# Four norms between the layers of a one-core kernel: pinned sums and spread, the residual feature by feature

## The chip, the core and the metric

The kernel runs on one core of one Trainium2 chip. The metric is the time of the device in microseconds for one execution. Engines are named as in the profile: PE (TensorE), DVE (VectorE), ACT (ScalarE), POOL (GpSimd) and SP (SyncE, which issues nearly all DMAs).

## The reference, cut to what matters

One batch of 512 tokens with 1024 features goes through four layers, the first two with 16 further tokens in front: a gated delta rule, a latent attention, a mixer of dilated attention and pooling, and a feed-forward layer. Each ends in an output projection, and behind each projection stands the same norm with a residual:

```python
def rmsnorm(x, g):
    xf = x.astype(jnp.float32)
    y = xf * lax.rsqrt(jnp.mean(xf * xf, axis=-1, keepdims=True) + NORM_EPS)
    return (y * g.astype(jnp.float32)).astype(x.dtype)
...
        h = h + rmsnorm(y, post_norm[layer])
```

The next layer starts with a norm of h and projections of it.

## The kernel before

All activations lie feature by feature: a partition is one of 128 features of a tile, eight tiles make the 1024 features, and tokens run along the free dimension, in two halves (272 and 256 tokens in the first joins' layer, 256 and 256 later). Every fp32 value is cut into a high and a low part (`hi` on ACT, `lo` on DVE or POOL, lines 70 to 80), and every product is three matmuls (lines 66 to 68): high by high, low by high, high by low. Weights come as raw tiles over SP and are cut in the same way (`whi` on ACT, `wlo` mostly on DVE).

A `Mix` is an output projection with its norm. There are four: of w_out (layer 1), w_out of layer 2, w_out of layer 3, and w_down. I call the passages behind the first three join 1, 2 and 3, and that behind w_down the end. A Mix runs column tile by column tile (m, eight of them) and half by half (i). ACT squares the result into `ysq` (line 339), POOL adds it to `acc` (line 341; the last tile's add is DVE's), and ACT writes the scaled result to `y` (line 342).

The norm of one half is `token_rs`: the sums, small matmuls of `acc` with ones (line 440); mean and eps on DVE (`v`, line 443); the power on POOL (line 446); a diagonal `dg` per 128 tokens on DVE (line 453); the spread, a matmul of ones with `dg` that puts a token's factor into all partitions (line 456); and a copy of it to SBUF, `rs`, on ACT (line 457). Then `residue` multiplies each feature of `y` by `rs` (line 367, even features on DVE, odd on POOL), adds the residual `resid` (line 369), and hands it to the next layer (`intake`: high and low part, scaled by the next norm's gain, as `h1hi`/`h1lo`, `x2hi`/`x2lo`, `x3hi`/`x3lo`). SP stores h to DRAM in two parts (line 375). Squares of h are added for the next norm (lines 467 to 471; POOL in half 0, DVE in half 1).

The residual of a half is one load of 1 MB (line 353) into one buffer: half 1's can start only when half 0's adds have read it.

While half 0 of a Mix is normed, PE goes on with column tiles of half 1. Sums and spread are issued by `Side`, a queue of steps with due times: each step of products moves its clock on by the time that PE should take (`PASS`), and a step that is due is traced at that place. `NORM_AFTER` and `NORM_GAP` are the due times of sums and spread in microseconds. In joins 2 and 3 the next layer's first four column tiles (PSUM tiles `first`) start early: `early()` runs them on half 0, one unit after another, and `late()` on half 1. The real order on each engine is set by a scheduler that simulates a timeline and takes instructions by readiness and priority; only what is marked with `keep_in_program_order` keeps its traced place.

Of the kernel before, what the change touches and what calls it, by code (L numbers as in the profile page):

```python
# [56 lines left out]
NORM_AFTER, NORM_GAP = 0.9, 2.0  # L57
# [7 lines left out]
def split_mm(nc, ps, whi, wlo, xhi, xlo, start, stop):  # L65
    nc.tensor.matmul(ps, lhsT=whi, rhs=xhi, start=start, stop=False)  # L66
    nc.tensor.matmul(ps, lhsT=whi, rhs=xlo, start=False, stop=False)  # L67
    nc.tensor.matmul(ps, lhsT=wlo, rhs=xhi, start=False, stop=stop)  # L68
# [136 lines left out]
def tile_model(ctx, tc, a, out):  # L205
# [7 lines left out]
    e.side = Side()  # L213
# [78 lines left out]
class Mix:  # L292
# [31 lines left out]
    def tile_parts(self, m, i, ks):  # L324
# [4 lines left out]
        for k, (hi, lo) in enumerate(ks):  # L329
            split_mm(nc, ps[:, :n], hi, lo, self.xhi[i][:, k], self.xlo[i][:, k], k == 0, k == len(ks) - 1)  # L330
# [6 lines left out]
        else:  # L337
            sq = pool.tile([P, self.hv[0].stop], F32, tag="ysq", name="ysq", bufs=2)
            nc.scalar.activation(sq[:, :n], ps[:, :n], AF.Square)  # L339
            eng = nc.vector if m == order[-1] else nc.gpsimd  # L340
            eng.tensor_tensor(out=acc[:, s], in0=acc[:, s], in1=sq[:, :n], op=ALU.add)  # L341
# [13 lines left out]
    def norm(self, i, nxt):  # L355
        e = self.e
        s = self.hv[i]
        rs = self.pool2.tile([P, self.hv[0].stop], F32, tag="rs", name="rs")[:, :s.stop - s.start]
        token_rs(e, rs, self.acc, s, D, NORM_AFTER, lambda: self.residue(i, nxt, rs), gap=NORM_GAP)

    def residue(self, i, nxt, rs):
        e, nc, y, x = self.e, self.e.nc, self.y[i], self.x[i]
        s = self.hv[i]
        n = s.stop - s.start
        for k in range(KT):
            eng = nc.gpsimd if k % 2 else nc.vector
            eng.tensor_tensor(out=y[:, k], in0=y[:, k], in1=rs, op=ALU.mult)  # L367
            eng = nc.gpsimd if nxt is None and k % 4 == 3 else nc.vector
            eng.tensor_tensor(out=y[:, k], in0=y[:, k], in1=x[:, k, :n], op=ALU.add)  # L369
            if nxt is None:  # L370
                nc.sync.dma_start(e.out[:, k, s], y[:, k])
            else:
                nxt.intake(k, i, s, y[:, k])
                if k % 4 == 3:
                    nc.sync.dma_start(self.h_dram[:, k - 3:k + 1, s], y[:, k - 3:k + 1])
        if nxt is not None:
            for k in range(KT):
                sum_squares(e, nxt.pool, nxt.acc, k, s, y[:, k])

# [1752 lines left out]
```

## Time and profile before

| | us |
|---|---|
| median of 3 runs | 1693.45 |
| lowest, highest run | 1687.04, 1695.97 |
| profiled execution | 1688.91 |
| its span, first to last instruction | 1687.1 |

| engine | busy us | share of the span |
|---|---|---|
| PE | 1592.0 | 94% |
| DVE | 992.4 | 59% |
| ACT | 836.1 | 50% |
| POOL | 470.9 | 28% |

The mean granted clock of TensorE over the span is 0.982. The joins lie at about 585 to 670, 1040 to 1097 and 1284 to 1331 us of the span, the end from 1655 on. A timeline row gives start and duration of a run of instructions and, in brackets, the idle time of the engine before it and what ended it; a row of waits gives the instruction that waited, what it waited for, the total, the number of times and the longest. A window's row gives the busy time of each engine in that stretch, with its number of instructions, and the granted clock.

### The profile page before, as it was taken

The numbers are of one execution on the slowest core, as the hardware profiler recorded it, in microseconds if no ns is written. First come the engines' busy times: TensorE is split into PE (matmuls) and PEld (weight loads), VectorE is DVE, ScalarE is ACT, GpSimd is POOL, SyncE is SP. The second block draws the span as 40 slices with busy tenths as digits, with TensorE's granted clock in tenths as the row PEclk, the third lists the DMA queues.
The fourth block names the chain that finished last, engine by engine and source line by source line (L and its number), as shares of the span: only waits on it lengthen the run. The fifth ranks groups of instructions, "written<-read, shape, count | busy, mean of one in ns | idle before, by whom it ended". The sixth has DMA issues, their size and how long they took to land.

```text
span 1687.1 us, 32900 instructions
## 1 busy us (share of the span) xinstructions
PE 1592.0 (94%) x12564; PEld 1456.0 (86%) x12564; DVE 992.4 (59%) x1944; ACT 836.1 (50%) x2005; POOL 470.9 (28%) x684
## 2 busy tenths in 40 slices
PE   6999869999999988999999999899998999999996
PEld 6999768888789988878999899788888888888996
DVE  6847749655365476785676623677855655554233
ACT  4876545544586553334666533435764433322230
POOL 1112110110286552122434312343535211111113
PEclk9999989999999998999999999999999999999998
DMA  3257963424466553456221223376624222223332
GB/s 134 95 174 209 199 153 123 119 85 157 132 178 197 176 193 105 142 186 192 59 76 48 73 94 132 119 233 192 159 69 140 88 94 94 100 98 105 98 113 76
DMA packets 133362, 219.72 MB, mean 130 GB/s; under 512 B 35989, under 2 KB 81365, under 8 KB 133077
## 3 DMA queue, kind: packets, MB, share of 16 engines
q1 hardware_dynamic: 126436, 204.83, 39.5%
q10 hardware_dynamic: 6768, 12.79, 2.1%
q8 instruction: 99, 1.62, 0.4%
q14 instruction: 59, 0.48, 0.1%
HBM read 173.81 MB, written 42.45 MB: 128 GB/s over the span
## 4 chain that ended last, share of the span: by engine, by line
PE 73%; DMA 8%; DVE 8%; issue 5%; ACT 4%; POOL 2%; SPq 1%; DVEq 0%; POOLq 0%; ACTq 0%
PE pj_t L66 19%; PE pj_t L67 19%; PE pj_t L68 19%; DMA bca<-row_a 2%; DMA item_dram<-bca 2%; DVE wlo L75 2%; DVE y L369 1%; DMA raw<-w_z 1%; DMA item<-item_dram 1%; DVE y L367 1%; PE ptr L1665 1%; PE ks L1234 1%; PE o_ps L1272 1%; PE sc L66 1%; PE ks L1233 1%
## 5 line engine op out<-in xcount | busy, mean ns | idle before, releaser
L75 DVE TENSOR_TENSOR wlo<-raw,whi 128x1024 fp32r<-128x1024 f32 (+2 forms) x218 | 290.5, 1334 | 239.2 <-ACT whi L74 238.6
L74 ACT ACTIVATE whi<-raw 128x1024 fp32r<-128x1024 f32 (+3 forms) x225 | 232.4, 1033 | 346.9 <-PE pj_t L67 205.1
L66 PE MATMUL pj_t<-hhi,whi 128*128 128x272 f32 (+2 forms) x760 | 224.3, 297 | 6.1 <-ACT y L665 1.9
L67 PE MATMUL pj_t<-hlo,whi 128*128 128x272 f32 (+2 forms) x760 | 223.8, 295 | 0.0
L68 PE MATMUL pj_t<-hhi,wlo 128*128 128x272 f32 (+2 forms) x760 | 223.2, 294 | 0.0
L66 PEld LDWEIGHTS pj_t<-hhi,whi 128*128 128x128 f32 (+1 forms) x760 | 145.2, 191 | 9.7 <-issue 2.6
L68 PEld LDWEIGHTS pj_t<-hhi,wlo 128*128 128x128 f32 (+1 forms) x760 | 145.0, 191 | 6.1 <-issue 5.5
L67 PEld LDWEIGHTS pj_t<-hlo,whi 128*128 128x128 f32 (+1 forms) x760 | 145.3, 191 | 2.5 <-issue 1.7
L68 PE MATMUL pj_t<-x3hi,wlo 128*128 128x512 f32 x320 | 124.6, 389 | 0.0
L66 PE MATMUL pj_t<-x3hi,whi 128*128 128x512 f32 x320 | 124.6, 389 | 0.0
L67 PE MATMUL pj_t<-x3lo,whi 128*128 128x512 f32 x320 | 124.5, 389 | 0.0
L341 POOL TENSOR_TENSOR acc<-acc,ysq 128x256 f32<-128x256 f32 (+1 forms) x48 | 58.4, 1217 | 194.8 <-ACT ysq L339 194.7
L68 PE MATMUL pj_t<-ahi,wlo 128*128 128x256 f32 x352 | 99.1, 282 | 0.0
L66 PE MATMUL pj_t<-ahi,whi 128*128 128x256 f32 x352 | 99.1, 282 | 0.0
L67 PE MATMUL pj_t<-alo,whi 128*128 128x256 f32 x352 | 99.0, 281 | 0.0
L1343 POOL TENSOR_SCALAR p<-p,st 128x144 f32<-128x144 f32 (+3 forms) x112 | 61.8, 553 | 132.5 <-DVE st L1342 91.4
L2022 POOL TENSOR_TENSOR gt<-gt,x3rs 128x512 f32<-128x512 f32 x22 | 30.1, 1368 | 191.6 <-DVE gt L2021 191.6
L68 PE MATMUL pj_t<-ghi,wlo 128*128 128x272 f32 (+1 forms) x256 | 74.1, 289 | 4.5 <-DVE wlo L75 4.5
L66 PE MATMUL pj_t<-ghi,whi 128*128 128x272 f32 (+1 forms) x256 | 75.8, 296 | 0.0
L1334 ACT ACTIVATE p<-p,st 128x144 f32<-128x144 f32 (+3 forms) x112 | 63.2, 564 | 23.2 <-DVE st L1329 21.1
L67 PE MATMUL pj_t<-h1lo,whi 128*128 128x512 f32 (+2 forms) x192 | 70.9, 370 | 3.4 <-DVE h1lo L75 2.9
L669 DVE SCALAR_TENSOR_TENSOR y<-xpad,fixed,y 128x528 f32<-128x528 f32 x96 | 73.4, 766 | 0.6
(551 smaller groups left out, 4797.0 us busy)
## 6 DMA issues: line engine op xcount, KB each, us to landing
raw<-w_out SPq DMA_DIRECT2D x54, 512.0 KB, 3.6
raw<-w_z SPq DMA_DIRECT2D x32, 512.0 KB, 3.3
item<-item_dram SPq DMA_DIRECT2D x32, 384.0 KB, 3.2
raw<-w_v SPq DMA_DIRECT2D x22, 512.0 KB, 4.0
raw<-w_gate SPq DMA_DIRECT2D x22, 512.0 KB, 3.2
raw<-w_up SPq DMA_DIRECT2D x22, 512.0 KB, 3.3
sz<-sz_dram SPq DMA_DIRECT2D x64, 128.0 KB, 2.7
raw<-w_down SPq DMA_DIRECT2D x16, 512.0 KB, 3.5
```

Of the source, the lines that this page charges most:

```text
L66: nc.tensor.matmul(ps, lhsT=whi, rhs=xhi, start=start, stop=False)
L67: nc.tensor.matmul(ps, lhsT=whi, rhs=xlo, start=False, stop=False)
L68: nc.tensor.matmul(ps, lhsT=wlo, rhs=xhi, start=False, stop=stop)
L74: nc.scalar.activation(hi, src, AF.Copy)
L75: (engine or nc.vector).tensor_tensor(out=lo, in0=src, in1=hi.bitcast(F32), op=ALU.subtract)
L341: eng.tensor_tensor(out=acc[:, s], in0=acc[:, s], in1=sq[:, :n], op=ALU.add)
L367: eng.tensor_tensor(out=y[:, k], in0=y[:, k], in1=rs, op=ALU.mult)
L369: eng.tensor_tensor(out=y[:, k], in0=y[:, k], in1=x[:, k, :n], op=ALU.add)
L669: nc.vector.scalar_tensor_tensor(out=y, in0=xpad[:, j:j + T1], scalar=cw[:, tap0, j:j + 1], in1=y, op0=ALU.mult, op1=ALU.add)
L1334: nc.scalar.activation(p[:, :at], p[:, :at], AF.Exp, bias=st[:, len(sc) - 1:len(sc)], scale=-1.0, accum_out=st[:, 3:4])
L1343: nc.gpsimd.tensor_scalar(out=p[:, :n], in0=p[:, :n], scalar1=st[:, 2:3], scalar2=factor, op0=ALU.mult, op1=ALU.mult)
L2022: nc.gpsimd.tensor_tensor(out=gt, in0=gt, in1=rs, op=ALU.mult)
```

## The change

Sums and spread of these norms are pinned: their matmuls, and the first matmul of the product behind them, keep the place on PE at which `Side` traced them, and both steps run at a raised priority (`NORM_EARLY`), as do the last column tile's square and add. `NORM_AFTER` goes from 0.9 to 1.3 and `NORM_GAP` from 2.0 to 2.2. ACT no longer copies the spread: the multiplications read it in PSUM, except in half 0 of the first Mix, where the copy stays.

`residue` becomes `features`: for each feature a multiplication, an add and (on ACT) the high part, then the low part of the feature before. All of it that is not ACT's is on DVE, in program order; POOL does none of it. In half 0 of the first Mix one feature is traced every 3.4 us (`FEATURE`) of the side queue's time; elsewhere all eight at once. `early` and `late` run the four first units feature by feature: all four with feature 0, then all four with feature 1. Their weights are taken before the last held tile of half 0.

```diff
-NORM_AFTER, NORM_GAP = 0.9, 2.0
+NORM_AFTER, NORM_GAP = 1.3, 2.2
+NORM_EARLY = 400
+FEATURE = 3.4
...
+    def place(self, ins):
+
+        self.tc.keep_in_program_order(ins)
+        self.held = True
+
+    def hold(self, ins):
+        if self.held:
+            self.tc.keep_in_program_order(ins)
+            self.held = False
...
+            last = m == order[-1]
+            with self.e.tc.high_priority(offset=NORM_EARLY if last else 0):
...
-        rs = self.pool2.tile([P, self.hv[0].stop], F32, tag="rs", name="rs")[:, :s.stop - s.start]
-        token_rs(e, rs, self.acc, s, D, NORM_AFTER, lambda: self.residue(i, nxt, rs), gap=NORM_GAP)
+        rs = None
+        if self.keep is None and i == 0:
+            rs = self.pool2.tile([P, CUT], F32, name="rs")[:, :s.stop - s.start]
...
+        steps = self.features(i, nxt, rs)
+        if self.keep is None and i == 0:
+            for j in range(KT + 1):
+                self.e.side.add(FEATURE * j, lambda: next(steps))
...
         for k in range(KT):
-            eng = nc.gpsimd if k % 2 else nc.vector
-            eng.tensor_tensor(out=y[:, k], in0=y[:, k], in1=rs, op=ALU.mult)
-            eng = nc.gpsimd if nxt is None and k % 4 == 3 else nc.vector
-            eng.tensor_tensor(out=y[:, k], in0=y[:, k], in1=x[:, k, :n], op=ALU.add)
+            in_order(nc.vector.tensor_tensor(out=y[:, k], in0=y[:, k], in1=rs, op=ALU.mult))
+            in_order(nc.vector.tensor_tensor(out=y[:, k], in0=y[:, k], in1=x[:, k, :n], op=ALU.add))
             if nxt is None:
                 nc.sync.dma_start(e.out[:, k, s], y[:, k])
-            else:
-                nxt.intake(k, i, s, y[:, k])
-                if k % 4 == 3:
-                    nc.sync.dma_start(self.h_dram[:, k - 3:k + 1, s], y[:, k - 3:k + 1])
+                continue
+            in_order(nxt.high(k, i, s, y[:, k]))
+            low()
+            low = lambda k=k: in_order(nxt.low(k, i, s, y[:, k]))
+            if k % 4 == 3:
+                nc.sync.dma_start(self.h_dram[:, k - 3:k + 1, s], y[:, k - 3:k + 1])
+            yield
...
+                if m == KT - 1 and nxt:
+                    nxt.take()
...
-            nc.tensor.matmul(ps[:, t:t + w], lhsT=e.ones, rhs=dg[:, :w], start=True, stop=True)
-        nc.scalar.activation(rs, ps[:, :n], AF.Copy)
-        then()
+            place(nc.tensor.matmul(ps[:, t:t + w], lhsT=e.ones, rhs=dg[:, :w], start=True, stop=True))
+        if rs is None:
+            then(ps[:, :n])
+        else:
+            nc.scalar.activation(rs, ps[:, :n], AF.Copy)
+            then(rs)
...
+def half_units(o, i):
+
     s = SEQ_HALVES[i]
     for k in range(KT):
         ks = slice(P * k, P * k + P)
-        split_mm(
-            o.e.nc, ps[:, s], unit[0][:, ks], unit[1][:, ks], o.hi[:, k, s], o.lo[:, k, s], k == 0, k == KT - 1
-        )
-        o.e.side.step((s.stop - s.start) * PASS)
+        for unit, ps in o.first:
+            split_mm(
+                o.e.nc, ps[:, s], unit[0][:, ks], unit[1][:, ks], o.hi[:, k, s], o.lo[:, k, s],
+                k == 0, k == KT - 1, o.e.side,
+            )
+            o.e.side.step((s.stop - s.start) * PASS)
```

On DVE in join 1, half 0, before: `y` is the Mix's result, `wlo` the low part of a weight tile for the running products of half 1. In brackets stands what an instruction waits for.

```order
L367 TENSOR_TENSOR y_6262<-y_6262,rs 128x272 [waits Activation_49]
L367 TENSOR_TENSOR y_6262<-y_6262,rs 128x272 x3
L369 TENSOR_TENSOR y_6262<-y_6262,resid 128x272 [waits DMAHW6_49,DVE_49]
L369 TENSOR_TENSOR y_6262<-y_6262,resid 128x272 [waits Pool_49]
L369 TENSOR_TENSOR y_6262<-y_6262,resid 128x272 [waits DVE_49] x2
L75 TENSOR_TENSOR wlo<-raw,whi 128x1024 [waits DMAHW7_49,PE_49,Activation_49]
L369 TENSOR_TENSOR y_6262<-y_6262,resid 128x272 [waits Pool_49]
```

The same place after:

```order
L402 TENSOR_TENSOR y_6262<-y_6262,rs 128x272 [waits Activation_49]
L403 TENSOR_TENSOR y_6262<-y_6262,resid 128x272 [waits DMAHW6_49,DVE_49]
L79 TENSOR_TENSOR wlo<-raw,whi 128x1024 [waits DMAHW5_49,PE_49,Activation_49]
L402 TENSOR_TENSOR y_6262<-y_6262,rs 128x272
L403 TENSOR_TENSOR y_6262<-y_6262,resid 128x272 [waits DVE_49]
L1492 TENSOR_TENSOR h1lo<-y_6262,h1hi 128x272 [waits Activation_49]
L79 TENSOR_TENSOR wlo<-raw,whi 128x1024 [waits DMAHW7_49,PE_49,Activation_49]
```

Each feature's multiplication and add now stand together, and a wlo stands behind one or two of them where it stood behind eight operations.

On DVE at the start of half 1 in join 2, before:

```order
L367 TENSOR_TENSOR y_12704<-y_12704,rs 128x256 [waits Activation_49]
L367 TENSOR_TENSOR y_12704<-y_12704,rs 128x256 x3
L369 TENSOR_TENSOR y_12704<-y_12704,resid 128x256 [waits DMAHW1_49,DVE_49]
L369 TENSOR_TENSOR y_12704<-y_12704,resid 128x256 [waits Pool_49]
L369 TENSOR_TENSOR y_12704<-y_12704,resid 128x256 [waits DVE_49] x2
L369 TENSOR_TENSOR y_12704<-y_12704,resid 128x256 [waits Pool_49]
L369 TENSOR_TENSOR y_12704<-y_12704,resid 128x256 [waits DVE_49]
L443 TENSOR_SCALAR v<-pj_t 128x2 [waits PE_49]
L369 TENSOR_TENSOR y_12704<-y_12704,resid 128x256 [waits Pool_49]
L78 SCALAR_TENSOR_TENSOR x2lo<-y_12704,fixed,x2hi 128x256 [waits Activation_49]
```

The same place after; `pj_t` is the PSUM tile with the spread:

```order
L402 TENSOR_TENSOR y_12702<-y_12702,pj_t 128x256 [waits PE_49]
L403 TENSOR_TENSOR y_12702<-y_12702,resid 128x256 [waits DMAHW1_49,DVE_49]
L402 TENSOR_TENSOR y_12702<-y_12702,pj_t 128x256
L403 TENSOR_TENSOR y_12702<-y_12702,resid 128x256 [waits DVE_49]
L1805 SCALAR_TENSOR_TENSOR x2lo<-y_12702,fixed,x2hi 128x256 [waits Activation_49]
L402 TENSOR_TENSOR y_12702<-y_12702,pj_t 128x256
L532 TENSOR_TENSOR x2acc<-x2acc,hsq 128x256 [waits Activation_49]
L501 TENSOR_SCALAR v<-pj_t 128x2 [waits PE_49]
```

The first low part moves from behind eleven operations to behind four.

On PE at the end of the first tiles in join 3, before, from the sums to the spread (`x3acc` holds the squares of h):

```order
L440 MATMUL pj_t<-ones,x3acc 128x1 [waits DVE_49,PE_49]
L440 MATMUL pj_t<-ones,x3acc 128x1
L66 MATMUL first<-x3hi,whi 128x256
L67 MATMUL first<-x3lo,whi 128x256
L68 MATMUL first<-x3hi,wlo 128x256
L66 MATMUL first<-x3hi,whi 128x256
```

Eight more such matmuls follow there before the spread. After:

```order
L72 MATMUL first<-x3hi,wlo 128x256
L497 MATMUL pj_t<-ones,x3acc 128x1 [waits DVE_49,PE_49]
L497 MATMUL pj_t<-ones,x3acc 128x1
L514 MATMUL pj_t<-dg_16921,ones 128x128 [waits DVE_49,PE_49]
L68 MATMUL pj_t<-x3hi,whi 128x512
```

Sums and spread now stand side by side behind the last of the first matmuls; in the norms of half 0 they come earlier than before, in join 2 the sums by 14 matmuls.

## Rows read from the trace of the kernel before

**Rows 1.** Waits of TensorE over the span: total us, times, longest us.

```profile
PE pj_t L456 <- DVE dg L453: 4.6, 4, 2.4
PE pj_t L68 <- DVE wlo L75: 4.5, 2, 3.2
...
PE first L66 <- ACT x3hi L77: 3.5, 1, 3.5
...
PE pj_t L67 <- DVE h1lo L75: 2.9, 1, 2.9
PE first L66 <- ACT x2hi L77: 2.9, 2, 2.2
PE pj_t L440 <- DVE acc L341: 2.4, 2, 1.4
PE first L67 <- DVE x2lo L78: 2.4, 2, 1.6
...
PE first L67 <- DVE x3lo L78: 1.0, 2, 0.9
```

**Rows 2.** Windows at the joins: us, busy time by engine, PEclk, DMA share, GB/s.

```profile
606.00:612.00 6.00, 4.20 (x23) 4.20 (x24) 6.00 (x6) 3.00 (x7) 5.84 (x6) 0.72 0.57 198
655.00:666.00 11.00, 9.54 (x46) 9.54 (x47) 6.03 (x18) 4.01 (x11) 1.76 (x2) 0.53 0.24 79
1056.00:1062.00 6.00, 3.71 (x29) 3.30 (x29) 6.00 (x14) 4.57 (x13) 2.11 (x4) 1.00 0.38 104
1076.00:1082.00 6.00, 5.16 (x24) 5.02 (x24) 5.52 (x17) 3.12 (x9) 0.82 (x1) 0.50 0.54 178
1082.00:1090.00 8.00, 8.00 (x69) 8.00 (x68) 2.71 (x6) 3.65 (x7) 0.00 (x0) 1.00 0.13 37
1297.00:1304.00 7.00, 6.08 (x28) 5.99 (x29) 7.00 (x17) 4.56 (x13) 4.04 (x5) 0.51 0.65 203
```

**Rows 3.** Timeline of VectorE in join 1, half 0.

```profile
593.91 3.23 DVE L367 TENSOR_TENSOR y<-y,rs 128x272 f32<-128x272 f32 x4 [1.25 <-ACT rs L457]
597.07 2.64 DVE L369 TENSOR_TENSOR y<-y,resid 128x272 f32<-128x272 f32 x4
599.63 1.80 DVE L75 TENSOR_TENSOR wlo<-raw,whi 128x1024 fp32r<-128x1024 f32 x1
601.36 3.76 DVE L369 TENSOR_TENSOR y<-y,resid 128x272 f32<-128x272 f32 x4
```

**Rows 4.** Timeline of VectorE, then of ScalarE, in join 2, half 1.

```profile
1070.54 3.05 DVE L367 TENSOR_TENSOR y<-y,rs 128x256 f32<-128x256 f32 x4 [3.11 <-ACT rs L457]
1073.51 2.61 DVE L369 TENSOR_TENSOR y<-y,resid 128x256 f32<-128x256 f32 x6
...
1074.48 0.51 ACT L77 ACTIVATE x2hi<-y,fixed 128x256 fp32r<-128x256 f32 x1 [3.98 <-DVE y L369]
```

**Rows 5.** The tile resid over the span: durations in ns, and its loads.

```profile
L369 DVE TENSOR_TENSOR y<-y,resid x60: 405/411/1012, 597.1 to 1682.5; 128x256 f32<-128x256 f32 x52, 128x272 f32<-128x272 f32 x8
...
DMA to landing us min/median/max: 5.7/6.5/7.6
```

**Rows 6.** Timeline of SyncE in join 2 and at the end.

```profile
1061.05 0.71 SPq L353 DMA_DIRECT2D resid<-h_w_out  x1
...
1672.99 0.53 SPq L353 DMA_DIRECT2D resid<-h_w_out  x1
1680.23 4.51 SPq L371 DMA_DIRECT2D out<-y  x8
```

**Rows 7.** Timeline of TensorE at the end of join 3.

```profile
1327.16 0.46 PE L456 MATMUL pj_t<-dg,ones 128*128 128x128 f32 x2 [0.59 <-DVE dg L453]
```

**Rows 8.** Timeline of VectorE at the end.

```profile
1676.32 3.01 DVE L367 TENSOR_TENSOR y<-y,rs 128x256 f32<-128x256 f32 x4 [1.17 <-ACT rs L457]
1679.26 3.67 DVE L369 TENSOR_TENSOR y<-y,resid 128x256 f32<-128x256 f32 x6
```

**Rows 9.** Groups of VectorE by line and form: count, busy us, mean ns, idle before.

```profile
L1690 DVE TENSOR_TENSOR sz<-pj_t,sz 128x256 f32<-128x256 f32 x32 | 13.1, 410 | 5.0 <-PE pj_t L68 5.0
```

More of the change, by code (lines that the diff above doesn't have):

```diff
@@ L62, with split_mm @@
 LOAD_AT = 1
-def split_mm(nc, ps, whi, wlo, xhi, xlo, start, stop):
-    nc.tensor.matmul(ps, lhsT=whi, rhs=xhi, start=start, stop=False)
+def split_mm(nc, ps, whi, wlo, xhi, xlo, start, stop, side=None):
+    first = nc.tensor.matmul(ps, lhsT=whi, rhs=xhi, start=start, stop=False)
+    if side is not None:
+        side.hold(first)
     nc.tensor.matmul(ps, lhsT=whi, rhs=xlo, start=False, stop=False)
@@ L337, in tile_parts @@
         else:
[L338 to L341, printed above, removed]
+            last = m == order[-1]
+            with self.e.tc.high_priority(offset=NORM_EARLY if last else 0):
+                sq = pool.tile([P, self.hv[0].stop], F32, tag="ysq", name="ysq", bufs=2)
+                nc.scalar.activation(sq[:, :n], ps[:, :n], AF.Square)
+                eng = nc.vector if last else nc.gpsimd
+                eng.tensor_tensor(out=acc[:, s], in0=acc[:, s], in1=sq[:, :n], op=ALU.add)
         nc.scalar.activation(self.y[i][:, m], ps[:, :n], AF.Copy, scale=self.e.vcol(self.gain, m))
@@ L401, in run @@
             e.wts.further(None)
+            e.wts.prefetch()
         else:
@@ L435, in token_rs, with first, _ahead @@
     v = e.small.tile([P, 4], F32, tag="v", name="v", bufs=2)
+    place = (lambda ins: None) if early is None else e.side.place
+    def first(step):
+        if early is None:
+            return step
+        return lambda: _ahead(step)
+    def _ahead(step):
+        with e.tc.high_priority(offset=early):
+            step()
     def sums():
@@ L439, in sums @@
         for j, (t, w) in enumerate(blocks):
-            nc.tensor.matmul(
-                ps[:, j:j + 1], lhsT=acc[:, s.start + t:s.start + t + P], rhs=e.ones[:, 0:1], start=True, stop=True
+            place(
+                nc.tensor.matmul(
+                    ps[:, j:j + 1], lhsT=acc[:, s.start + t:s.start + t + P], rhs=e.ones[:, 0:1], start=True, stop=True
+                )
             )
@@ L446, in sums @@
         nc.gpsimd.tensor_tensor(out=v[:, :nb], in0=v[:, :nb], in1=e.half_pow[:, :nb], op=ALU.pow)
-        e.side.add(gap, spread)
+        e.side.add(gap, first(spread))
     def spread():
@@ L1391, in late_units @@
         token_rs(o.e, o.rs[:, s], o.acc, s, D, delay, gap=LATE_GAP)
-    for m in range(len(o.first)):
-        half_unit(o, m, 1)
+    half_units(o, 1)
     o.e.wts.prefetch()
-def half_unit(o, m, i):
-    unit, ps = o.first[m]
+def half_units(o, i):
     s = SEQ_HALVES[i]
@@ L1987, in open, with high, low, take @@
         self.rs = pool.tile([P, SEQ], F32, name="x3rs")
-    def intake(self, k, i, s, h):
+    def high(self, k, i, s, h):
         if self.pool is None:
             self.open()
-        cut(self.e.nc, self.hi[:, k, s], self.lo[:, k, s], h, self.e.vcol("pre_ffn", k))
+        return self.e.nc.scalar.activation(self.hi[:, k, s], h, AF.Copy, scale=self.e.vcol("pre_ffn", k))
+    def low(self, k, i, s, h):
+        return self.e.nc.vector.scalar_tensor_tensor(
+            out=self.lo[:, k, s], in0=h, scalar=self.e.vcol("pre_ffn", k), in1=self.hi[:, k, s].bitcast(F32),
+            op0=ALU.mult, op1=ALU.subtract,
+        )
+    def take(self):
+        take_units(self, [(n, m) for m in range(2) for n in ("w_gate", "w_up")])
     def early(self):
-        early_units(self, [(n, m) for m in range(2) for n in ("w_gate", "w_up")])
+        half_units(self, 0)
     def late(self):
```

56 lines of the change are left out of this document (39 added, 17 removed).

## The prediction

> **What bounds the kernel now.** I read the waits of TensorE first, then the windows with the granted clock, then VectorE's and ScalarE's timelines at the joins between layers. TensorE's waits at the joins are what this change can touch: 4.5 us for wlo in join 1 (after w_out0), 2.4 us for the squares' sum acc, 2.9 us for h1lo, 2.9 and 2.4 us for x2hi and x2lo in join 2 (after w_out1), 3.5 and 1.0 us for x3hi and x3lo in join 3 (after w_out3), and 4.6 us in all for dg before the spread [rows 1]. That makes 24.2 us.
>
> A second cost follows the longest of them. [...] Each gives up its length times what lacks to 1: 6 x 0.28 = 1.7, 11 x 0.47 = 5.2, 6 x 0.50 = 3.0, 7 x 0.49 = 3.4 us, 13.3 us together. The stretch from 1056 to 1062 stands against them: it holds waits of about 0.7 and 1.6 us for x2hi and x2lo, and its clock is 1.00 [rows 1, 2]. So short waits leave the clock alone, and taking a wait below that size gives back more than the wait.
>
> Why TensorE waits is in VectorE's order. Before, one half's residue runs as four multiplications, then all adds, and only then what the next product needs. In join 1 VectorE is busy without a break from 593.9 to 605.1 with multiplications, adds and one wlo, and the wlo that TensorE's running product needs stand between and behind them [rows 3]. In join 2 the four multiplications start at 1070.5 and the adds at 1073.5; the first x2hi comes at 1074.5, because the adds of every feature stand behind all multiplications [rows 4]. Four multiplications take VectorE 3.05 us there, 0.76 each, while GpSimd does the other four; the median of VectorE's adds of this size is 0.411 [rows 4, 5]. So one hand needs 3.3 us for eight, against some 3.1 to 3.6 with two.
>
> **The change, part by part.** *Join 1, half 0.* The features now come one per 3.4 us of TensorE's time, with the wlo between them in VectorE's order. A wlo then waits for at most one multiplication and one add (2 x 0.411 = 0.8 us; before, 2.6 and 3.8 us of adds stood ahead of it) [rows 3, 5]. It is needed no sooner than before, so I count the whole 4.5 us and the 1.7 us of clock: 6.2 us, bounds 4 and 6.5 (one remaining wait of 0.8 twice, or none). Eight features at 3.4 us take 27 us; half 1's eight column tiles of w_out0, 8 x 48 matmuls x 0.116 = 45 us, cover them before anything reads h1.
>
> *Join 1, half 1.* The sums wait there behind two wlo (1.4 of the 2.4 us for acc). Pinning moves the sums up by some matmuls and raises the squares' priority, but VectorE still has the wlo in hand, so the wait stays as it is or grows by 0.3 us: cost -0.3. Behind the spread one feature needs a multiplication, an add, a high part on ScalarE, and the low part of the feature before, so low parts are ready one by one instead of after all adds. The wait for h1lo, 2.9 us, falls to about 1 in all, and the 5.2 us of clock go with it: 2.9 - 1.0 + 5.2 - 0.3 = 6.8 us, bounds 3 (the clock falls all the same for half of the time) and 8.
>
> *Join 2.* Half 0: its features now end before TensorE arrives, since sums and spread come some 14 matmuls earlier (1.6 us) and the first high part after two operations instead of after eight. The 0.7 and 1.6 us go: 2.3 us. Half 1: the multiplication reads the spread in PSUM, so ScalarE's copy of rs goes, and hi comes 2 x 0.411 later instead of 4.0 us after the first multiplication [rows 4, 5]. What is next late is the residual: its load is issued at 1061.05 [rows 6] and loads of this size take 5.7 to 7.6 us [rows 5]; one buffer serves both halves, so it still waits for half 0's last add. It lands at 1067 to 1069; the first low part can stand at 1069 to 1070.2, and TensorE, whose 96 matmuls of half 0 take 11.1 us from about 1057 and the sums and spread between them about 1.4, arrives at 1069.5. Wait left: 0.7 us, bounds 0 and 2. From there eight features cost VectorE four operations each (multiplication, add, low part, squares' add), 4 x 0.411 = 1.64 us, against 12 matmuls, 12 x 0.116 = 1.4 us, on TensorE: 0 to 8 x 0.24 = 1.9 us; I take 0.8, as successive VectorE operations partly overlap. The clock's 3.0 us go. At the end sums and spread now stand directly behind each other, as they do before: 2.4 us stays 2.2. Sum: 2.9 + 2.4 + 3.0 + 0.2 - 0.7 - 0.8 = 7.0 us, bounds 4 and 9.
>
> *Join 3.* The same with x3: 3.5 + 1.0 + 3.4 us go; left are 1 us for the residual and 0.8 us for VectorE. The end is worse than before: there 12 matmuls stood between sums and spread and hid most of the chain (sums, v, pow, dg), and now none does. I take the 2.2 us of join 2, whose wait for dg is the longest with 2.4 [rows 1], where 0.6 was paid [rows 7]: -1.6. Sum: 7.9 - 1.8 - 1.6 = 4.5 us, bounds 2 and 6.
>
> *End.* Before, the multiplications start at 1676.32, the adds end at 1679.26 + 3.67 = 1682.9 [rows 8], and stores are issued until 1680.23 + 4.51 = 1684.7, the residual's load only at 1672.99 behind half 0's stores [rows 6]. After, the copy of rs goes, so the first multiplication starts near 1675.8; 16 operations of 0.411 end at 1682.4, each store is issued as its feature ends, and the last by 1683.0. Half 0's stores no longer wait for GpSimd: its 16 operations take VectorE 6.6 us and start with the earlier spread, so the load is issued some 3 us sooner and lands in time. Gain 1.7 us, bounds -0.5 (the load still lands at 1679) and 3.
>
> *At nothing.* Taking weights earlier, the moved prefetch and the constants NORM_AFTER and NORM_GAP: the cuts are the same in number, beside the same products; if their cover went, one wlo (1.80 us [rows 3]) would show. GpSimd loses 44 operations and keeps pow and the sums of half 0.
>
> *A price for reading PSUM.* A VectorE operation of this size with an input in PSUM (sz, line 1690) takes 0.410 us, the same as an add from SBUF [rows 5, 9]. So the sum holds no price for it. [...]
>
> **The sum.** 6.2 + 6.8 + 7.0 + 4.5 + 1.7 = 26.2 us. From the profiled execution's 1688.9 us (span 1687.1 and 1.8 around it) this gives 1662.7; from the median of 1693.45, which is 4.5 above, 1667.3. I start all cases from the middle of the two, 1691.2: 1665. By the bounds the gain is 12.5 to 32.5 us, so 1656 to 1681 across both bases.
>
> **Rivals.** [...]
>
> *VectorE becomes the bound.* It takes over 44 operations, pinned in order: one that waits (for ScalarE's high part, for PSUM) stops wlo and v behind it. If a feature takes 2.0 us instead of 1.64, three second halves lose 3 x 8 x 0.36 = 8.6 us, and 4 more in late wlo: gain 13.6, time 1678. For it: VectorE is busy 6.00 of 6 us from 1056 and 5.52 of 6 from 1076; against it, only 2.71 of the 8 us after 1082, into which the same work can spread [rows 2].
>
> *It doesn't do what it says.* The scheduler gave the matmuls of features the same order, or the residual's landing holds half 1 of each join as long as the adds did: gain 6 in join 1 and little else, 1685. The order of instructions speaks against the first, the load times [rows 5] against the second.
>
> *Slower: pinned sums and spread stop TensorE.* Eight pairs now stand at fixed places. If VectorE or GpSimd is later than that place by as much as the longest wait for wlo, 3.2 us [rows 1], and the clock then falls for 3.4, six such places cost 6 x 6.6 = 40 us: 1691.2 - 26.2 + 40 = 1705. It decides from about 5 such places on. Against it: sums to dg takes 2.4 us at its longest [rows 1], and except at the ends about 20 matmuls (2.4 us) lie between.
>
> **How the numbers follow.** Forecast 0.62 (its own range 1656 to 1674), clock 0.14, VectorE 0.09, little done 0.09, slower 0.06. The first three are over 0.5% faster (below 1685; 0.5%, 8.5 us, is about what a measurement here can tell from no change): 0.85; within 0.5%, 0.09; slower, 0.06. The range takes the forecast, clock and VectorE: 1655 to 1682.
>
> **What would show it.** Right: no wait for wlo near 600 and 607; clock 1.00 from 606 to 612, 655 to 666 and at both later joins; x2hi and x3hi starting about 1 us after the multiplication; the first wait of half 1 ended by the residual. Wrong: waits over 2 us for x2lo or x3lo inside the features, a clock near 0.5 in any join, a wait over 3 us at the end of join 3, or stores at the end paced by the load.

## The result

The changed kernel takes 1665.41 us (median of 4 runs, 1662.06 to 1670.78) against 1693.62 us (4 runs, 1687.04 to 1695.97): a ratio of 0.984, 95% interval 0.980 to 0.988. Faster, by 28.2 us of the medians; the forecast was a gain of 26.2 us, and 1665 us from its base of 1691.2. The profiled execution took 1664.7 us with a span of 1662.8, 24.3 us less than the span before. The total came out as forecast; several of its terms did not.

To see the terms I cut each trace at the starts of the last matmuls of certain kinds, which both kernels run in the same order. Join 1 is cut at the last matmul of `state`, of `ghi` by `wlo`, and of the sums of `lsq`; joins 2 and 3 at the last matmul of the layer's own projection (`g1hi`, `mhi`), then at the last of `first` (a), then at the last product of `x2hi` or `x3hi` with a `wlo` behind it (b); the end runs from the last matmul of w_down to the end of the span. The rest of the span is in the last column.

| us | join 1, half 0 | join 1, half 1 | join 2 a | join 2 b | join 3 a | join 3 b | end | sum | rest |
|---|---|---|---|---|---|---|---|---|---|
| before | 74.6 | 49.8 | 33.6 | 94.9 | 33.0 | 218.8 | 15.3 | 520.0 | 1167.1 |
| after | 67.3 | 44.1 | 24.7 | 98.8 | 27.3 | 222.2 | 13.8 | 498.1 | 1164.7 |
| after, again (first experiment) | 67.3 | 44.1 | 24.7 | 98.4 | 27.4 | 222.2 | 13.7 | 497.8 | 1172.3 |

The stretches repeat to 0.4 us between two executions of the changed kernel, while the rest differs by 7.6 us. So the change itself is worth 21.9 us; of the 24.3 us between the two profiled spans 2.4 are the rest, and so are some of the 28.2 between the medians.

The waits of TensorE in the changed kernel that answer to [rows 1] (total, times, longest); those for wlo, h1lo, x2hi, x2lo and x3lo are gone. Of the three for dg, 2.4 and 2.0 us stand at the ends of joins 2 and 3:

```profile
PE pj_t L514 <- DVE dg L511: 5.9, 3, 2.4
...
PE pj_t L497 <- DVE acc L361: 2.8, 2, 1.8
...
PE first L68 <- ACT x3hi L2065: 2.3, 1, 2.3
```

The windows that answer to [rows 2], moved by the time gained (busy time of PE, weight loads, DVE, ACT, POOL; PEclk; DMA):

```profile
601.00:607.00 6.00, 6.00 (x53) 6.00 (x53) 4.93 (x7) 4.57 (x10) 3.70 (x4) 1.00 0.83 274
629.00:637.00 8.00, 6.22 (x39) 6.13 (x38) 4.26 (x8) 1.36 (x2) 0.71 (x1) 0.79 0.17 67
640.00:651.00 11.00, 11.00 (x96) 11.00 (x96) 10.10 (x32) 6.22 (x18) 1.97 (x1) 1.00 0.29 95
1041.00:1055.00 14.00, 14.00 (x120) 14.00 (x119) 9.36 (x24) 5.97 (x16) 5.01 (x7) 1.00 0.56 172
1066.00:1070.00 4.00, 1.57 (x13) 1.51 (x12) 2.31 (x5) 2.00 (x2) 1.62 (x1) 0.83 0.36 109
1070.00:1076.00 6.00, 6.00 (x33) 6.00 (x31) 3.29 (x4) 1.44 (x2) 1.61 (x1) 0.55 0.55 193
...
1304.00:1308.00 4.00, 4.00 (x13) 3.11 (x12) 0.05 (x1) 0.00 (x0) 0.00 (x0) 0.57 0.67 234
```

A further window lies inside join 2 b, some 47 us behind its sums:

```profile
1116.00:1120.00 4.00, 3.26 (x16) 3.29 (x17) 3.60 (x13) 2.82 (x8) 1.97 (x3) 0.57 0.95 337
```

Where the first wlo was late (600 to 607), where h1 was taken in (640 to 651) and where x2's half 0 and the start of half 1 run (1041 to 1055), TensorE is now busy for the whole stretch at full clock. The half clock (a granted clock of 0.50, as from 1076 to 1082 before [rows 2]) has not gone: it stands, over part of each window, behind the sums of join 1, half 1 (0.79), behind the end of join 2's first units (0.83 and 0.55) and behind that of join 3's (0.57). A fourth place (0.57 from 1116 to 1120) is new: TensorE had just waited 2.3 us there for pt of the attention. The kernel before waits 2.1 us for pt in this stretch as well, and its clock reads 1.00 all the way from 1090 to 1186.

VectorE in join 1, half 0, answering to [rows 3]: a wlo now stands behind the two or three operations of one feature.

```profile
591.01 1.22 DVE L79 TENSOR_TENSOR wlo<-raw,whi 128x1024 fp32r<-128x1024 f32 x1 [1.09 <-ACT whi L78]
592.16 0.43 DVE L402 TENSOR_TENSOR y<-y,rs 128x272 f32<-128x272 f32 x1
592.63 0.44 DVE L403 TENSOR_TENSOR y<-y,resid 128x272 f32<-128x272 f32 x1
592.99 0.43 DVE L1492 TENSOR_TENSOR h1lo<-y,h1hi 128x272 fp32r<-128x272 f32 x1
593.34 1.22 DVE L79 TENSOR_TENSOR wlo<-raw,whi 128x1024 fp32r<-128x1024 f32 x1
```

VectorE at the start of half 1 in join 3: the first multiplication is done, then VectorE waits 5.07 us for the residual, issued at 1280.71. TensorE's 2.3 us for x3hi above are the visible part of that.

```profile
1281.67 0.42 DVE L402 TENSOR_TENSOR y<-y,pj_t 128x256 f32<-128x256 f32 x1
1287.16 0.42 DVE L403 TENSOR_TENSOR y<-y,resid 128x256 f32<-128x256 f32 x1 [5.07 <-DMA resid<-h_w_out]
```

VectorE at the end of join 2's first units: v waits for the sums, a cut of weights (wlo) runs while GpSimd computes the power, then dg; TensorE's spread starts at 1069.50 after 2.43 us idle.

```profile
1067.11 0.16 DVE L501 TENSOR_SCALAR v<-pj_t 128x2 f32<-128x2 f32 x1 [2.81 <-PE pj_t L497]
1067.25 1.23 DVE L79 TENSOR_TENSOR wlo<-raw,whi 128x1024 fp32r<-128x1024 f32 x1
1069.07 0.48 DVE L511 TENSOR_SCALAR dg<-fixed,v 128x128 f32<-128x128 f32 x2 [0.59 <-POOL v L504]
```

At the end, SyncE's last stores answer to [rows 6]; the residual of half 1 is issued at 1646.18, 7.4 us ahead of the first multiplication at 1653.61 (before, 3.3):

```profile
1646.18 0.53 SPq L373 DMA_DIRECT2D resid<-h_w_out  x1
1654.52 5.87 SPq L405 DMA_DIRECT2D out<-y  x8
```

TensorE's spread there, before and after:

```profile
1675.10 0.68 PE L456 MATMUL pj_t<-dg,ones 128*128 128x128 f32 x4 [1.45 <-DVE dg L453]
```

```profile
1652.38 1.19 PE L514 MATMUL pj_t<-dg,ones 128*128 128x128 f32 x4 [1.45 <-DVE dg L511]
```

### The profile page after: what moved, and what is told of

Its sections match the earlier page's. It is cut to its first block, busy times and chain, and to the rows that moved or that the text cites. A ratio compares the mean times of both kernels' runs of the same rounds, so it can differ in the third digit from the quotient of the medians.

```text
span 1662.8 us, 32878 instructions
## 1 busy us (share of the span) xinstructions
PE 1585.1 (95%) x12564; PEld 1452.0 (87%) x12564; DVE 985.6 (59%) x1988; ACT 834.5 (50%) x1998; POOL 434.2 (26%) x640
## 4 chain that ended last, share of the span: by engine, by line
PE 74%; DMA 10%; DVE 6%; ACT 4%; issue 4%; POOL 1%; SPq 0%; POOLq 0%; ACTq 0%; DVEq 0%
PE pj_t L68 20%; PE pj_t L71 19%; PE pj_t L72 19%; DMA bca<-row_a 2%; DMA item_dram<-bca 1%; DVE wlo L79 1%; DMA bc<-row_b 1%; DMA raw<-w_z 1%; PE ptr L1729 1%; ACT whi L78 1%; PE first L68 1%; PE first L71 1%; PE sc L68 1%; PE first L72 1%; PE vtp L1143 1%
## 5 line engine op out<-in xcount | busy, mean ns | idle before, releaser
L71 PE MATMUL pj_t<-glo,whi 128*128 128x272 f32 (+1 forms) x256 | 72.8, 284 | 0.0
```

## The experiments

Theory A said that the gain comes from VectorE's order, with what TensorE needs next ready feature by feature. Theory B, its rival, said that it comes from the sums and spread, pinned and earlier. All experiments are edits of the changed kernel. Since the rest of the span moved by 7.6 us between two executions of the same kernel, more than most of the effects, the verdicts rest on the stretches:

| us | join 1, half 0 | join 1, half 1 | join 2 a | join 2 b | join 3 a | join 3 b | end | sum |
|---|---|---|---|---|---|---|---|---|
| no order | 71.5 | 46.2 | 29.9 | 96.1 | 30.1 | 218.0 | 13.4 | 505.1 |
| no pin | 68.1 | 43.8 | 29.0 | 93.8 | 32.0 | 220.6 | 14.1 | 501.3 |
| by unit | 67.3 | 45.3 | 24.7 | 97.1 | 27.3 | 222.2 | 13.8 | 497.6 |
| early sums | 67.3 | 44.4 | 25.4 | 93.9 | 28.0 | 218.9 | 13.8 | 491.6 |
| split residual | 67.3 | 46.2 | 24.7 | 96.7 | 25.0 | 218.9 | 13.7 | 492.5 |
| both | 67.3 | 46.3 | 25.1 | 94.1 | 25.0 | 218.9 | 13.8 | 490.4 |
| all at once | 70.4 | 45.9 | 24.7 | 97.8 | 27.0 | 222.2 | 13.8 | 501.6 |
| combined | 67.3 | 44.3 | 25.1 | 93.8 | 25.0 | 218.9 | 13.6 | 488.0 |
| no order, no pin | 74.3 | 41.0 | 29.7 | 95.8 | 31.8 | 218.3 | 13.9 | 504.7 |
| copy and GpSimd back | 67.3 | 46.5 | 27.3 | 93.7 | 28.1 | 222.2 | 14.4 | 499.3 |
| all three undone | 73.9 | 43.8 | 35.5 | 97.6 | 32.8 | 218.0 | 14.6 | 516.1 |

Not all of the rest is untouched. From the end of join 1 to the start of join 2 the kernel before takes 369.8 us, the changed one 369.9 and 370.5. The two edits that do not reach join 1 leave 369.7 (by unit) and 371.6 (early sums), no order 370.4 and all three undone 371.2; the others lengthen it, to 371.8 (combined) up to 374.0 (copy and GpSimd back) and 374.2 (split residual). Each is one execution. Where an edit reaches join 1, the stretches may thus understate its price by up to some 4 us.

**The changed kernel again.** 

> The changed kernel once more, unaltered, as the yardstick for the three beside it. 1662 to 1671 us as in its four runs so far. If the half clock behind the waits at the ends of joins 2 and 3 is a fixed effect of those waits (2.7 and 2.5 with 2.3 us), the stretches right after them show it again; if it also hangs on something that changes from run to run, one of them is missing or a new one appears elsewhere.

1669.16 us (1663.21 to 1671.91). The half clock came back in the same places, the three at the joins and the one behind pt. It is tied to what happens there, but see the run without pin below.

**No order.**

```diff
-        in_order = e.tc.keep_in_program_order
+        in_order = lambda ins: ins
```

> The changed kernel with one edit: the operations of the features on VectorE and ScalarE no longer keep their program order, so all eight multiplications come first, then all adds, then the low parts. Theory A (the gain comes from VectorE's order: what TensorE needs next is ready feature by feature): TensorE waits again for the high and low parts at the start of both halves in joins 2 and 3 and for wlo in join 1, 15 us or more of the 24 are lost, 1680 us or more. Theory B (the gain comes from the pinned sums and spread and from the copy that went): at most 5 us are lost, 1670 us or less.

1674.14 us, the stretches 7.2 us longer. Between the two expectations: the waits came back, but smaller, that for wlo with 1.0 us. In join 1 the sums of half 1 wait 3.9 us, more than in the kernels before and after. The waits of TensorE in this run, and VectorE at the start of half 1 in join 2:

```profile
PE pj_t L497 <- DVE acc L361: 5.0, 2, 3.9
...
PE first L71 <- DVE x3lo L2068: 3.0, 2, 1.6
...
PE first L71 <- DVE x2lo L1805: 1.5, 1, 1.5
```

```profile
1063.07 2.74 DVE L402 TENSOR_TENSOR y<-y,pj_t 128x256 f32<-128x256 f32 x8 [2.33 <-PE pj_t L514]
1065.72 2.10 DVE L403 TENSOR_TENSOR y<-y,resid 128x256 f32<-128x256 f32 x6
```

With GpSimd out of the way eight multiplications take VectorE 2.74 us, 0.34 each, where four took 3.05, 0.76 each, in [rows 4]. VectorE alone does all eight in less time than the two engines did together, and so the old order hurts less than it did before. That these read the spread in PSUM is not the reason: in join 1, half 0 of the same run the eight read the copy in SBUF, and 272 columns take 0.36 us each.

```profile
592.92 2.91 DVE L402 TENSOR_TENSOR y<-y,rs 128x272 f32<-128x272 f32 x8 [1.62 <-ACT rs L518]
```

**No pin.**

```diff
     def place(self, ins):
-        self.tc.keep_in_program_order(ins)
-        self.held = True
+        pass
```

> The changed kernel with one edit: the matmuls of sums and spread are no longer pinned (they keep the raised priority and the due times). Theory A: the spread of half 0 comes a dozen matmuls later in joins 3 and at the end; half 0 has slack, so the loss is 0 to 3 us, 1665 to 1668 us. Theory B: the loss is 8 us or more, 1673 us or more.

1674.02 us, but the stretches only 3.4 us longer: join 2 a and join 3 a lose 4.3 and 4.7 us, and 4.8 and 1.6 come back behind them. The time alone would have spoken for Theory B; the rest was 1169.9. Theory A's loss of 0 to 3 us is missed by a little, and its place was wrong. In join 2 TensorE waits 2.5 us for an x2hi, which it does not in the changed kernel, and the window behind, 1065 to 1069, reads 0.58; in join 3 the spread came ahead of features and stopped TensorE for 1.4 us, and 1294 to 1302 reads 0.57. One thing in this run matters for the clock. The end of join 2's first units again waits 2.4 us, from 1078.2 to 1080.6, and the window over it and behind it reads:

```profile
1077.00:1090.00 13.00, 10.56 (x89) 10.38 (x88) 9.35 (x16) 4.81 (x7) 5.48 (x4) 1.00 0.47 162
```

The clock is full, where the same wait in the changed kernel was followed by 0.55.

**By unit.**

```diff
-    for k in range(KT):
-        ks = slice(P * k, P * k + P)
-        for unit, ps in o.first:
+    for unit, ps in o.first:
+        for k in range(KT):
+            ks = slice(P * k, P * k + P)
```

> The changed kernel with one edit: the four first units of joins 2 and 3 run one after another again, each over all eight features, in both halves. Theory A: the first unit needs all eight features within 24 matmuls (2.8 us) while VectorE makes one in 1.4 to 1.6 us, so in half 1 TensorE waits up to 8 us per join for them and gets back, at most, the wait for the spread at the end (2.3 to 2.7 us), which the last unit then covers; in all a loss of 5 to 12 us, 1670 to 1677 us. Rival C (the scheduler reorders the matmuls by readiness anyway, so that the written order does not matter): within 2 us of the changed kernel.

1665.9 us, the stretches within 0.5 us of the changed kernel, joins 2 a and 3 a within 0.1. Rival C holds: the written order of the units carries nothing, as it would if the scheduler takes these matmuls by readiness. My expectation was wrong. The run also shows how far a stretch moves that an edit does not reach: join 1's half 1 is 1.2 us longer, where the sums wait 3.0 us instead of 1.8.

**Early sums.**

```diff
-LATE_AFTER, LATE_GAP = (0.5, 7.0), 5
+LATE_AFTER, LATE_GAP = (0.5, 6.0), 5
...
-        token_rs(o.e, o.rs[:, s], o.acc, s, D, delay, gap=LATE_GAP)
+        token_rs(o.e, o.rs[:, s], o.acc, s, D, delay, gap=LATE_GAP, early=NORM_EARLY)
```

> The changed kernel with two edits: the norm's sums and spread behind the first units of joins 2 and 3 are pinned too, and the second sums come earlier, some 12 matmuls before the end of the first units instead of behind them. The stretches are compared by the trace, since the layers ahead of the joins differ by some us from run to run. Theory A (the wait at the end of the first units, 2.7 and 2.3 us, and the half clock that follows it give back the gain of joins 2 and 3): both waits fall to about 1.3 us, no half clock follows, and the stretches behind the first units get shorter by 3 to 5 us (join 2) and 2 to 3.5 us (join 3). Rival D (VectorE's cut of a weight tile between v and dg sets the end, or the pinned sums only move the wait forward to the squares): both stretches together gain under 2 us.

1662.29 us. Behind the first units 4.8 us came back in join 2 and 3.3 in join 3, for 0.7 more in each at the units themselves. TensorE's spreads there, and the windows over and behind them:

```profile
1069.34 0.49 PE L514 MATMUL pj_t<-dg,ones 128*128 128x128 f32 x2 [0.37 <-DVE dg L511]
```

```profile
1299.31 0.71 PE L514 MATMUL pj_t<-dg,ones 128*128 128x128 f32 x4 [0.61 <-DVE dg L511]
```

```profile
1068.00:1072.00 4.00, 3.63 (x31) 3.42 (x30) 2.62 (x4) 0.93 (x2) 0.47 (x1) 1.00 0.79 266
1072.00:1078.00 6.00, 6.00 (x51) 5.87 (x50) 5.70 (x10) 2.14 (x4) 3.04 (x2) 1.00 0.46 137
1298.00:1301.00 3.00, 2.39 (x15) 1.99 (x15) 2.74 (x5) 1.98 (x3) 0.14 (x1) 1.00 0.29 91
1301.00:1308.00 7.00, 7.00 (x32) 5.80 (x31) 5.35 (x8) 4.93 (x9) 2.54 (x2) 1.00 0.33 113
```

The waits fall to 0.4 and 0.6 us, the clock stays full, and join 3 b is back at 218.9, the 218.8 of before. The 3.4 us that join 3 b had lost are thus the wait and the clock behind it. The half clock behind pt in join 2 b stays (now from 1114.0). Rival D falls.

**Split residual.**

```diff
+        parts = self.x.setdefault(i, [None, None])
+        for p in range(2) if part is None else (part,):
+            x = parts[p] = self.pool2.tile([P, KT // 2, self.hv[0].stop], F32, tag=f"resid{p}", name="resid")
...
             if k % 4 == 3:
                 nc.sync.dma_start(self.h_dram[:, k - 3:k + 1, s], y[:, k - 3:k + 1])
+                if i == 0 and self.keep is not None:
+                    self.fetch(1, part=k // 4)
```

> The changed kernel with one edit: the residual of a half is two loads of 0.5 MB into two buffers, and half 1's first part is issued as soon as half 0's first four features have read theirs. Theory A (in join 3 the residual's landing is the last wait of half 1): the wait of VectorE for it, 5.1 us, is gone, TensorE's wait of 2.3 us for x3hi falls below 0.5 us, and the stretch of join 3's first units gets 2 us shorter; join 2, where TensorE did not wait for it, stays within 0.3 us. Rival E (VectorE's chain of features alone keeps TensorE waiting): join 3's stretch stays within 0.5 us.

1667.76 us. Join 3 a is 2.3 us shorter and TensorE's wait for x3hi is gone. VectorE there waits for the spread alone:

```profile
1286.63 0.42 DVE L404 TENSOR_TENSOR y<-y,pj_t 128x256 f32<-128x256 f32 x1 [0.29 <-PE pj_t L518]
1287.08 0.43 DVE L405 TENSOR_TENSOR y<-y,resid 128x256 f32<-128x256 f32 x1
```

Join 2 a stays the same, as expected. Rival E falls. Join 3 b gained 3.3 us too: with half 1 earlier, the scheduler moved the sums ahead of the last matmuls. Not expected: join 1's half 1 got 2.1 us longer, where the sums' wait for acc grew:

```profile
PE pj_t L501 <- DVE acc L361: 4.6, 2, 3.6
```

**Both.** 

> Both edits of the two kernels before in one. Theory A: the gains add, 4 us at the first units and behind them in join 3 and 3 to 5 us in join 2, 7 to 9 us in all against the changed kernel, about 1658 us where that has 1666. If half 1 of join 3 then runs at VectorE's pace, a part of the 2 us from the residual does not come.

1662.49 us. The stretches are 7.4 us shorter than the changed kernel's second execution: 3.9 in join 2, 5.7 in join 3, less 2.1 for the longer join 1. They do not add, since each edit alone had already mended the end of join 3.

**All at once.**

```diff
-FEATURE = 3.4
+FEATURE = 0.0
```

> The changed kernel with one constant set to 0: in half 0 of join 1 all eight features are traced at once instead of one per 3.4 us. Theory A: the sixteen operations and the low parts then stand ahead of the cuts again, in feature order (8 x 1.25 = 10 us of VectorE), so the waits for wlo near 600 come back: join 1's half 0 loses 4 to 7 us of the 7.3 that it gained. Theory B (the spacing does not matter, since the pinned order was enough): under 1 us.

1676.01 us (5 runs). Join 1 loses 3.1 us in half 0 and 1.7 in half 1, less than expected but far from nothing. A wait for wlo is back, and in half 1 the sums wait longer for acc:

```profile
PE pj_t L497 <- DVE acc L361: 4.9, 2, 3.9
...
PE pj_t L72 <- DVE wlo L79: 1.9, 2, 1.7
```

Of the 7.3 us of half 0 the order without the spacing keeps 4.2; the spacing gives the other 3.1. (1177.9 of the span is the untouched rest, 5.6 us more than in the first experiment, so the time overstates it.)

**Combined.** The early sums, the split residual except in the first Mix, and:

```diff
-                eng = nc.vector if last else nc.gpsimd
+                eng = nc.vector if last and (self.keep is not None or i == 0) else nc.gpsimd
```

> The changed kernel with three edits: the pinned early sums behind the first units; the residual split in two loads in the Mixes that hold weights back (w_out of layers 2 and 3, w_down) and whole in the first; and in half 1 of join 1 the last square added on GpSimd instead of VectorE. Theory A for the last one: the sums of join 1's half 1 wait for an add that stands behind a scaling and a cut of weights on VectorE, 2.0 us, with half a clock behind it; on GpSimd, idle there, the add is done about 2 us sooner, and join 1's second half gets 2 to 4 us shorter than the changed kernel's 44.1. The joins 2 and 3 as in the run with both edits: 4 and 5.5 us shorter, and no lengthening of join 1 as the split load brought there. About 1656 us where the changed kernel has 1666. Rival F: GpSimd's add takes 1.2 us and more and the spread then waits for it instead; join 1 gains under 1 us.

1656.67 us (1652.09 to 1659.74), a ratio of 0.977 (0.972 to 0.981) to the kernel before: 37 us faster than it, and 9 us faster than the median of the changed kernel. The stretches are 9.8 us shorter than the changed kernel's. All of it is in joins 2 and 3; join 1's half 1 stayed at 44.3, so Rival F holds in its outcome, though not for its reason: the add takes GpSimd 0.88 us, the sums no longer wait and end at 630.6, but v then stands on VectorE behind a scaling and a cut of weights until 633.2, and TensorE waits 1.3 us for the spread:

```profile
634.60 0.46 PE L523 MATMUL pj_t<-dg,ones 128*128 128x128 f32 x2 [1.28 <-DVE dg L520]
```

```profile
632.06 1.21 DVE L79 TENSOR_TENSOR wlo<-raw,whi 128x1024 fp32r<-128x1024 f32 x1
633.19 0.15 DVE L510 TENSOR_SCALAR v<-pj_t 128x2 f32<-128x2 f32 x1
```

The clock falls there later, behind a wait of 0.9 us for lsq at 645.62:

```profile
640.00:655.00 15.00, 14.14 (x107) 13.94 (x107) 10.61 (x33) 7.81 (x21) 1.97 (x1) 0.89 0.29 91
```

**No order, no pin.** The first two edits in one.

> The changed kernel with neither the features' order nor the pinned sums and spread; it keeps the priority, the removed copy, the work moved from GpSimd to VectorE, and the written order of the first units. If order and pin make the gain together and stand in for each other in part, the stretches of the joins lose more than the two single undoings did together (about 7 and 5 us), 15 us or more, 1681 us or more. If they are independent, 12 us. If the rest of the change carries the gain, under 8 us.

1673.7 us, the stretches 6.9 us longer than in the changed kernel: no more than without the order alone. It kept 15.3 of the 22 us. This was the result that Theory A could not take: without order and without pin most of the gain was still there. In join 1's half 1 it even runs 3.1 us shorter than the changed kernel: the unpinned sums wait for nothing. In the other two runs without pins they wait 0.7 and 1.1 us, in the pinned ones 1.8 to 3.9 as long as VectorE makes the last add, so that in this place the pin costs time, 5.2 us without the order (46.2 against 41.0) and 0.4 with it.

**Copy and GpSimd back.**

```diff
-        rs = None
-        if self.keep is None and i == 0:
-            rs = self.pool2.tile([P, CUT], F32, name="rs")[:, :s.stop - s.start]
+        rs = self.pool2.tile([P, CUT], F32, tag="rs", name="rs")[:, :s.stop - s.start]
...
-            in_order(nc.vector.tensor_tensor(out=y[:, k], in0=y[:, k], in1=rs, op=ALU.mult))
+            eng = nc.gpsimd if k % 2 else nc.vector
+            in_order(eng.tensor_tensor(out=y[:, k], in0=y[:, k], in1=rs, op=ALU.mult))
```

> The changed kernel with ScalarE's copy of the spread back in all halves and the odd features' multiplications back on GpSimd, both in the features' order. Theory A: the chain to the first high part gets 0.5 us longer for the copy, and multiplications on either engine take 0.8 us while both run (0.42 on VectorE alone), so a feature waits for GpSimd about as long as before; joins 2 and 3 lose 1 to 3 us together, the end 1 to 2 us. Theory G (taking the work from GpSimd was a burden that the order had to make up for): the joins' stretches get shorter.

1672.87 us, but the stretches lose just 1.5 us: join 1's half 1 2.3, join 2 a 2.6, join 3 a and the end 0.7 each, with 4.7 back behind join 2, where the spread's wait was 1.4 us and the clock stayed full:

```profile
1081.00:1176.00 95.00, 90.30 (x528) 79.37 (x528) 67.97 (x124) 43.30 (x85) 36.08 (x34) 1.00 0.69 209
```

So where the work stands it costs some 6 us, and the clock, which the changed kernel loses in join 2 b and this run does not, gives most of it back. Behind join 1 TensorE has a new wait for qt with half clock behind it (0.57 from 686 to 690), and the passage up to join 2 is 3.5 to 4.1 us longer, which the stretches leave out:

```profile
PE pj_t L68 <- DVE qt L1582: 2.1, 1, 2.1
```

That sharing with GpSimd is cheap once the order is kept is thus not shown.

**All three undone.**

> The changed kernel without the features' order, without the pinned sums and spread, and with ScalarE's copy and the odd multiplications on GpSimd back; what is left of the change is the raised priority, the spacing and due times, the weights taken early and the low parts on VectorE. The run without order and pin kept 14 of the 22 us that the joins' stretches gave. If the removed copy and the work taken from GpSimd carry these 14, the joins and the end lose 10 us more, 1684 us or more. If what is left carries them, it stays within 4 us of that run, 1670 to 1678 us. Undoing copy and GpSimd alone cost the stretches 5 us, so I expect something between, 1679 us.

1686.02 us (10 runs), a ratio of 0.996 (0.994 to 0.998); the stretches are at 516.1, 18.3 us above the changed kernel and 3.9 below the kernel before. The waits of TensorE, beside [rows 1], and VectorE in join 2's half 1, which is [rows 4] again:

```profile
PE pj_t L72 <- DVE wlo L79: 3.6, 2, 3.4
PE first L68 <- ACT x3hi L2063: 3.5, 1, 3.5
PE first L68 <- ACT x2hi L1800: 3.0, 2, 2.2
PE first L71 <- DVE x2lo L1803: 2.8, 2, 1.6
```

```profile
1066.54 3.05 DVE L400 TENSOR_TENSOR y<-y,rs 128x256 f32<-128x256 f32 x4 [3.08 <-ACT rs L516]
1069.51 2.61 DVE L401 TENSOR_TENSOR y<-y,resid 128x256 f32<-128x256 f32 x6
```

So the three parts carry 18 of the 22 us, and by the stretches they stand in for each other. Order and pin are worth 6.9 us while VectorE works alone (504.7 against 497.8) and 16.8 while GpSimd shares and ScalarE copies (516.1 against 499.3). The other way round, VectorE alone without the copy is worth 1.5 us with the order and 11.4 without it (516.1 against 504.7).

Most of that difference of 9.9 us is the clock and not the order. 6.6 of it lie in join 2 b, where by the granted clock of each trace half clock costs 5.1 us in the changed kernel, 1.7 without order and pin, nothing with copy and GpSimd back and 3.4 with all three undone. What is left is in join 2 a: order and pin are worth 5.0 us there with VectorE alone (29.7 against 24.7) and 8.2 with GpSimd sharing (35.5 against 27.3). These 3.2 us speak for two ways to have the first high part in time, one feature after the other, or all eight multiplications at once at 0.34 us, and against Theories A and B as they stood. With the passage between joins 1 and 2 counted in, the three undone singly cost 7.3, 5.9 and 5.0 us, 18.2 in sum, and 18.9 together; order and pin together then cost 8.9 where they cost 13.2 singly. That order and pin replace each other in part holds by either count; that the third part replaces them is not shown.

## Why the prediction was right, and where it was not

- **Join 1, half 0** (6.2 us forecast, 7.3 measured). Right in mechanism: both waits for wlo and the half clock went. The upper bound of 6.5 was too low. The run with all features at once shows that the spacing carries 3.1 of it. A wlo stands behind up to three operations of a feature, not two, and TensorE waits for none.
- **Join 1, half 1** (6.8, measured 5.7). Right on h1lo, whose wait is gone without the 1 us that I left for it. The wait of the sums stayed, 1.8 us where it was 1.4, as I had said; but I priced nothing for the clock behind it, and 629 to 637 reads 0.79, that is 8 x 0.21 = 1.7 us.
- **Join 2** (7.0, measured 5.0). Here the first step failed, "short waits leave the clock alone". The first units gain 8.9 us, more than I summed for them, since VectorE's features cost TensorE nothing and the residual did not hold it either. But 3.9 us went again behind them: the wait at the end is as long as before, 2.4 us, and this time the clock fell after it, to which the sum gave no price. The windows 1066 to 1076 give 4 x 0.17 + 6 x 0.45 = 3.4 us, and the one behind pt, 1116 to 1120, 4 x 0.43 = 1.7 more; 1.2 us came back elsewhere in the stretch. The early sums, which take the wait away, win back the loss behind it.
- **Join 3** (4.5, measured 2.4). The end was rightly said to get worse, and the wait is 2.0 us as priced (2.2); the clock behind it, 4 x 0.43 = 1.7 us, was again not. The residual was named as the next to be late, but at 1 us; it was 2.3.
- **The end** (1.7, measured 1.6). Right in size; of the mechanism the half that counts. The first multiplication starts 4.6 us behind the last product, as before, and not 0.5 us sooner: the copy is gone, but the four matmuls of the spread took 1.19 us, at half clock (0.50 from 1652.4 to 1653.5), where they had taken 0.68 at full clock (1.00 from 1675.1 to 1675.8). The gain is in the stores, whose issuing now ends 0.4 us behind the last add, where it ended 1.8 behind.
- **Nothing for the PSUM source.** Multiplications from PSUM took 0.416 us (median of 56), the adds, both inputs in SBUF, 0.425 (median of 64); right.
- **The total.** The terms of the sum came to 26.2 us against 21.9 measured in their places: 4.3 too many. The 13.3 us of clock counted as regained are the lengths of the four stretches of [rows 2] that read 0.72, 0.53, 0.50 and 0.51, times what each lacks to 1; by the windows 1.7 + 3.4 + 1.7 + 1.7 = 8.5 us of clock are still lost in joins 1 to 3; the waits gave some 4 us more than their terms. The medians' 28.2 us hide this, since the other layers happened to differ as well, and so does the base of 1691.2, which lies 2.4 below the median. That the time met the forecast within 0.4 us is in part luck. The 0.116 us per matmul in the terms is 8.00 us over the 69 from 1082 to 1090 [rows 2]; those of 256 columns start 0.12 us apart, before (1089.79 to 1090.63, seven times) and after (1113.08 to 1114.16, nine times).
- **Of the rivals,** the clock (chance 0.14: many short waits, one at each feature, bring the half clock as the long ones had, 5.2 + 3.0 + 3.4 us stay lost and the time is 1677) came true in part, for a cause that I had not named: not the short waits of the features, of which none is left in join 2, but one wait at the end of each join and one for pt, which the kernel before had too. Clock 1.00 at both later joins, named as a sign of being right, was not seen, and a clock near 0.5 in any join, named as a sign of being wrong, was (0.55 and 0.57). VectorE did not become the bound; pinned sums and spread stopped TensorE only where the stop had been before or was priced.

Open is why the wait of 2.4 us at the end of join 2 is followed by half clock in the changed kernel, and not in the kernel before or without the pin. It hangs on more than the length of one wait; no run here tells on what.

## What to carry to other kernels

When an engine off the critical path makes what the next product needs, have it finish one piece before it starts the next, and put the pieces of two consumers (here features and weight cuts) in turn. Judge a part of a change by undoing it together with the others as well as alone: here order and pin cost 7.2 and 3.4 us of the stretches when undone singly and 6.9 when undone together. Cut the trace where the effect ends, and look at the clock in every stretch before a sum is read as a mechanism: the passage behind join 1, which no stretch here holds, moved by up to 4 us, and half clock came and went with 5 us in join 2. And after such a change look at the next wait in line, here the chain from sums to spread and the residual's load: mending both took another 10 us from the stretches.

## What the runs showed of the hardware

Sharing short operations of 128 x 256 between VectorE and GpSimd gained nothing: eight independent multiplications take VectorE 0.34 us each while GpSimd does none, 2.74 in all (no order), and 0.76 each for four while GpSimd does the other four in 3.58 (before, and again with all three undone). Operations of a feature that depend on each other start about 0.46 us apart (at the end of the changed kernel 1653.61 and 1654.07), independent ones 0.34 (1654.07 and 1654.41).

A wait of TensorE of 2.4 us at the end of join 2's first units was followed by half clock in the changed kernel (0.55 from 1070 to 1076; join 2 b took 98.8 and 98.4 us in its two executions), and by full clock in the kernel before (1.00 from 1090 to 1186) and without the pin (1.00 from 1077 to 1090). And while the joins repeated to 0.4 us between two executions of the changed kernel, the rest of the span moved by 7.6 us, 0.6 of it between joins 1 and 2; a difference of some us in the time is not yet one of the change.
